# Fourteen units of the first layer's weights: the high and the low part made by GpSimd's casting and adding transfers instead of a VectorE subtraction

## The chip, the cores and the metric

The kernel runs on one core of one Trainium2 chip. The metric is the time of one launch on the device, in microseconds (us): the median of several executions. A profiled execution has its own time, and a span (first to last recorded instruction) that is a little shorter.

## The reference

A trunk of two layers over 256 latent tokens (a grid of 4 rows by 64) and 256 context tokens, both 1024 wide. What matters here is the first sub-layer, in which one projection feeds three branches:

```python
h = modulate(rmsnorm(x, norm1_g[l]), sh1, sc1)          # adaLN, the context stream likewise
p = h @ w_in[l]                                          # columns: a, g | q, k, v | gates
u = a * sigmoid(g); u = dwconv1d(u, dw, dw_b)            # 31 taps, depthwise
y_conv = silu(layernorm(u)) @ w_conv_out[l]
y_attn = merge_heads(neighbourhood_attention(q, k, v, k_c, v_c, rpb[l])) @ w_na_out[l]
x = x + g1 * (sigmoid(p_gc) * y_conv + sigmoid(p_ga) * y_attn) @ w_out[l]
```

The second sub-layer is a gated MLP (2816 wide) with a depthwise convolution of width 3. In the first layer the context tokens go through all of it as well, so its products run over 512 columns (256 latent, 256 context); in the second layer nearly all run over 256. All is fp32.

## The kernel before, in words

**Weights.** All weights of a layer lie in DRAM as 118 *units* of 128 partitions x 1024 fp32 (512 KB), each of them eight 128x128 tiles. Every product is made exact enough by splitting both operands into a high part in TensorE's type `fp32r` and the rest: `mm3` (L178) issues three matmuls per tile, high weight by high input (L179), high weight by low input (L180), low weight by high input (L181). A unit takes 24 matmuls of 128x512 in the first layer.

**Loading a unit** (`wparts` L150, `wunit` L170). SyncE (SP) issues one DMA into a `raw` tile (L157). ScalarE copies `raw` into `whi`, which rounds it to `fp32r` (L160). VectorE writes `wlo = raw - whi` (L161). `raw`, `whi` and `wlo` have four buffers each, which rotate; a buffer is taken again when the last reader of its old content is done. So the cast of a unit waits for the last L180 of the unit four places back, and the subtraction for its last L181. `unit8` (L193) returns the eight tile pairs of a unit, and `group` (L183) runs the 24 products of an output tile.

**The order of the work.** The program is written in the order in which TensorE is to work; the Tile framework then schedules each engine's instructions in an order of its own from that, and sets the waits. Every engine works through its list in order, so an instruction that waits holds up all behind it on the same engine. DMAs are issued by the engine on whose list they stand. Work of other kinds is put between the products by generators that `slot()` steps on (convolution taps, attention, adaLN products).

**Layer 0 up to the gates**, in the order of TensorE's work:

- x is loaded and its squares are summed; the adaLN rows for the first shift and scale come from products with the `wada` weights (L203, `sil` by `raw`). Then, for k = 0 to 7, `modulated` (L357) makes the high part of h on ScalarE (L366, 256 columns at a time) and the low part on VectorE (L367). TensorE makes the V products (L644) of that k and one or two GLU products of the first two GLU tiles (`glu0` L696, in the `sc` banks), and behind them the adaLN products for k+1.
- The 14 units U_IN to U_IN+13 follow in this order: Q0, K0, a1, g1, Q1, K1, a2, g2, Q2, K2, a3, g3, Q3, K3 (`qk` L749, `glu_groups` L617), with `in_group` (L614) calling `unit8`. Unit 14, the first gate (`gate` L624), is next and then 15 more of them. For Q and K, VectorE applies the rotation (L762 to L765), ScalarE makes their high part (L768) and VectorE the low part (L769); a Q also loads its bias of 640 KB (L760).
- Between those groups runs the attention (class at L385). A step makes the scores (L440) into the two `sc` banks and into `pt` and `main`; VectorE adds the bias and takes the row's minimum (L458); ScalarE takes the exponential (L461) and divides by the sum (L464). Some groups later `turn` (L486) transposes the probabilities on TensorE (L494, L499), ScalarE copies them out of PSUM into `pT` (L495 latent, L500 context), and `values` (L504) multiplies with V. PSUM has four `main` banks, two `sc`, one `pt`, one `po`.
- VectorE also does the convolution's taps (L589, L591), two per slot, each 128x512. `layer_norm` (L832) starts when all four tiles `cb_0` to `cb_3` are done; its first two sums are on GpSimd (L842 of `cb_0` and `cb_1`, L843).
- Later come adaLN dot products on VectorE (L271) with a row `sb` that is loaded by SP (L253) and goes through SiLU on ScalarE (L255).

GpSimd does little: memsets at the start, the powers for the norms' roots (L346), and L842/L843. It issues no DMA in the kernel before.

Of the kernel before, what the change touches and what calls it, by code (L numbers as in the profile page):

```python
# [8 lines left out]
F32 = mybir.dt.float32  # L9
F32R = mybir.dt.float32r  # L10
BF16 = mybir.dt.bfloat16
AF = mybir.ActivationFunctionType
ALU = mybir.AluOpType
AX = mybir.AxisListType

P = 128
# [15 lines left out]
UW = 1024  # L32
# [5 lines left out]
U_GLU0, U_V, U_IN, U_NA, U_CO, U_WO, U_UP, U_DN = 0, 2, 6, 36, 40, 44, 52, 96  # L38
# [7 lines left out]
def trunk(ctx: ExitStack, tc: tile.TileContext, xt, cvec, crow, wall, wada, params, bias_t, rope_t, out):  # L46
    nc = tc.nc
    pe, act, dve, pool, sp = nc.tensor, nc.scalar, nc.vector, nc.gpsimd, nc.sync
# [4 lines left out]
    wp = ctx.enter_context(tc.tile_pool(name="w", bufs=1))  # L53
# [6 lines left out]
    def nm(s):  # L60
        uid[0] += 1
        return f"{s}_{uid[0]}"
# [80 lines left out]
    lastdma = [None]  # L143
# [6 lines left out]
    def wparts(l, u, at=None, cuts=2):  # L150

        r = wp.tile([P, UW], F32, tag="raw", bufs=4, name=nm("raw"))
        hi = (at or wp).tile([P, UW], F32R, tag="whi", bufs=4, name=nm("whi"))
        lo = (at or wp).tile([P, UW], F32R, tag="wlo", bufs=4, name=nm("wlo"))
        cs = [slice(i * UW // cuts, (i + 1) * UW // cuts) for i in range(cuts)]
        for c in cs:
            lastdma[0] = sp.dma_start(r[:, c], wall[l, u][:, c])  # L157

        def split(c):
            act.copy(hi[:, c], r[:, c])  # L160
            dve.tensor_tensor(lo[:, c], r[:, c], hi[:, c].bitcast(F32), ALU.subtract)  # L161

        def more():
            for c in cs[1:]:
                split(c)

        split(cs[0])
        return (hi, lo), more

    def wunit(l, u, at=None, cuts=1):  # L170
        w, more = wparts(l, u, at, cuts)
        more()
        return w

    def cols(w, i):
        return sl(w[0], i), sl(w[1], i)
# [6 lines left out]
    def group(ps, ws, xh, xl, c):  # L183
# [6 lines left out]
        slot()  # L190
        return ps

    def unit8(l, u, at=None):  # L193
        w = wunit(l, u, at)
        return [cols(w, i) for i in range(KD)]


# [360 lines left out]
    for l in range(DEPTH):  # L558
# [5 lines left out]
        with ExitStack() if last else start as e1a:  # L564
# [49 lines left out]
            def in_group(t, c, tag="main"):  # L614
                return group(psum(tag), unit8(l, U_IN + t), *h1, c)
# [17 lines left out]
            with ExitStack() as e1b:  # L633
# [15 lines left out]
                if l == 0:  # L649
# [27 lines left out]
                    def more():  # L677
                        act.copy(wg[0][:, cuts[0]], rg[:, cuts[0]])
                        act.copy(pb, ps)
                        act.copy(wv[0][:, cuts[1]], rv[:, cuts[1]])  # L680
                        act.copy(wg[0][:, cuts[1]], rg[:, cuts[1]])
                        for w, r, c in ((wv, rv, cuts[0]), (wg, rg, cuts[0]), (wv, rv, cuts[1])):
                            low_part(w, r, c)
# [132 lines left out]
            with ExitStack() as e1c:  # L816
# [108 lines left out]
                for n in range(NB):  # L925
                    ps = group(psum(), unit8(l, U_WO + n), *z, ALL)
                    for s in range(NS):
                        residual(sss[s], ps, 2, n, s, s * S)
                    if last:
                        plain(n)  # L930
                    elif n == 0:
                        pace[0] = 0.8
                pace[0] = 0.3
                held = [unit8(l, U_WO + n) for n in range(NB, KD)]
                for s in range(NS if held else 0):
                    for n, w in zip(range(NB, KD), held):
# [13 lines left out]
        with ExitStack() as e2:  # L950
# [45 lines left out]
            if last:  # L996
# [14 lines left out]
                for i, ps in enumerate(pss):  # L1011
                    b = small([P, 1], "wb", 4)
                    act.copy(b, ps[:, S : S + 1])
                    u = ef.tile([P, S], F32, name=f"u{l}_{i}")
# [32 lines left out]
            for i in range(2, KF):  # L1047
                w = [unit8(l, ups[2 * i + t]) for t in range(2)]
# [176 lines left out]
```

## Time and profile before

| | |
|---|---|
| median of 3 runs | 1128.44 us (1127.71 to 1128.83) |
| the profiled execution | 1127.64 us, its span 1125.9 us |
| granted TensorE clock, mean | 0.998 of full speed |
| TensorE's weight loads (beside its matmuls) | 963.0 us busy, 86% of the span |
| moved by DMA | 190.83 MB, 169 GB/s over the span |

The profile puts every instruction under the source line that issued it. A row of groups names the line, the engine, the operation and its tiles as out<-in, how many there are (x244), their busy time and the mean of one in ns, then the engine's idle time just before them and who ended most of it. PE is TensorE, PEld its weight loads, DVE VectorE, ACT ScalarE, POOL GpSimd, SP SyncE; a q behind the name of an engine is its queue, which issues DMAs. A row of the order of time begins with the start of an instruction and its duration, both in us, and ends, in brackets, with the idle time before it and its releaser. For a DMA the second number is the time from issue to landing in the list of transfers, and the issue's own in the list of instructions. A row of windows gives, behind its bounds, the length of the stretch and each engine's busy time in it.

### The profile page before, as it was taken

The numbers are of one execution on the slowest core, as the hardware profiler recorded it, in microseconds if no ns is written. First come the engines' busy times: TensorE is split into PE (matmuls) and PEld (weight loads), VectorE is DVE, ScalarE is ACT, GpSimd is POOL, SyncE is SP. The second block draws the span as 40 slices with busy tenths as digits, with TensorE's granted clock in tenths as the row PEclk, the third lists the DMA queues.
The fourth block names the chain that finished last, engine by engine and source line by source line (L and its number), as shares of the span: only waits on it lengthen the run. The fifth ranks groups of instructions, "written<-read, shape, count | busy, mean of one in ns | idle before, by whom it ended". The sixth has DMA issues, their size and how long they took to land.

```text
span 1125.9 us, 17731 instructions
## 1 busy us (share of the span) xinstructions
PE 1114.1 (99%) x6828; PEld 963.0 (86%) x6828; DVE 908.3 (81%) x1631; ACT 563.6 (50%) x934; POOL 14.7 (1%) x24
## 2 busy tenths in 40 slices
PE   9999999999999999999999999999999999999997
PEld 7778777787789988888888888989888999999997
DVE  5689999685778788888898555789996898988773
ACT  4347657542333543434343222544677667766642
POOL 0000000000000000000000000000000000000000
PEclk9999999999999999999999999999999999999999
DMA  9833231536734354554556665556433575565781
GB/s 364 282 94 103 75 118 38 206 97 214 245 118 138 114 161 150 168 169 149 168 171 215 219 191 186 180 181 187 145 126 121 167 250 163 188 194 181 219 268 58
DMA packets 53941, 190.83 MB, mean 169 GB/s; under 512 B 6240, under 2 KB 6496, under 8 KB 53856
## 3 DMA queue, kind: packets, MB, share of 16 engines
q1 hardware_dynamic: 53568, 189.65, 52.1%
q8 instruction: 54, 0.88, 0.3%
q14 instruction: 31, 0.25, 0.1%
q10 hardware_dynamic: 288, 0.04, 0.0%
HBM read 188.62 MB, written 1.05 MB: 168 GB/s over the span
## 4 chain that ended last, share of the span: by engine, by line
PE 83%; DVE 9%; issue 6%; ACT 2%; DMA 0%; POOL 0%; POOLq 0%; DVEq 0%; SPq 0%; ACTq 0%
PE main L179 24%; PE main L181 24%; PE main L180 24%; DVE cb L591 4%; PE main L644 4%; DVE wlo L161 1%; PE sc L181 1%; PE sc L179 1%; PE sc L180 1%; PE po L202 1%; PE po L512 1%; PE sc L129 1%; PE sc L440 0%; DMA sb<-in_crow 0%; PE sc L494 0%
## 5 line engine op out<-in xcount | busy, mean ns | idle before, releaser
L179 PE MATMUL main<-h,whi 128*128 128x256 f32 (+1 forms) x1328 | 446.7, 337 | 0.0
L181 PE MATMUL main<-h,wlo 128*128 128x256 f32 (+1 forms) x1328 | 442.9, 335 | 1.0 <-DVE wlo L161 1.0
L180 PE MATMUL main<-h,whi 128*128 128x256 f32 (+1 forms) x1328 | 442.2, 334 | 0.1
L160 ACT CAST whi<-raw 128x1024 fp32r<-128x1024 f32 (+1 forms) x244 | 252.3, 1039 | 285.5 <-PE main L180 131.5
L161 DVE TENSOR_TENSOR wlo<-raw,whi 128x1024 fp32r<-128x1024 f32 (+1 forms) x244 | 292.9, 1207 | 112.5 <-ACT whi L160 108.0
L179 PEld LDWEIGHTS main<-h,whi 128*128 128x128 f32 x1328 | 249.4, 188 | 32.1 <-issue 3.6
L181 PEld LDWEIGHTS main<-h,wlo 128*128 128x128 f32 x1328 | 249.3, 188 | 29.6 <-DVE wlo L161 1.5
L180 PEld LDWEIGHTS main<-h,whi 128*128 128x128 f32 x1328 | 249.8, 188 | 28.5 <-DVE h L367 0.5
L591 DVE SCALAR_TENSOR_TENSOR cb<-u,par,cb 128x512 f32<-128x512 f32 (+1 forms) x240 | 140.4, 609 | 1.4
L271 DVE CUSTOM_DVE_ANT_0 t<-raw,sb,par 128x1024 bf16<-128x1024 f32 x100 | 126.7, 1277 | 1.0 <-ACT sb L255 0.7
L179 PE MATMUL main<-fh,whi 128*128 128x256 f32 (+1 forms) x386 | 123.0, 319 | 0.0
L180 PE MATMUL main<-fl,whi 128*128 128x256 f32 (+1 forms) x386 | 122.9, 319 | 0.0
L181 PE MATMUL main<-fh,wlo 128*128 128x256 f32 (+1 forms) x386 | 122.9, 318 | 0.0
L180 PEld LDWEIGHTS main<-fl,whi 128*128 128x128 f32 x386 | 72.7, 188 | 5.6
L179 PEld LDWEIGHTS main<-fh,whi 128*128 128x128 f32 x386 | 72.7, 188 | 5.6
L181 PEld LDWEIGHTS main<-fh,wlo 128*128 128x128 f32 x386 | 72.7, 188 | 5.5
L963 ACT ACTIVATE t<-main,par 128x512 f32<-128x512 f32 (+1 forms) x82 | 50.6, 667 | 39.0 <-PE main L181 39.0
L964 DVE SCALAR_TENSOR_TENSOR t<-main,par,t 128x510 f32<-128x510 f32 (+1 forms) x82 | 47.5, 615 | 10.2 <-ACT t L963 9.8
L967 DVE SCALAR_TENSOR_TENSOR t<-main,par,t 128x510 f32<-128x510 f32 (+1 forms) x82 | 46.6, 609 | 0.0
L366 ACT ACTIVATE h<-t,mod 128x256 fp32r<-128x256 f32 x56 | 25.4, 502 | 36.1 <-DVE t L365 36.1
L898 DVE SCALAR_TENSOR_TENSOR x<-main,mod,x 128x256 f32<-128x256 f32 x48 | 22.1, 479 | 23.5 <-PE main L181 23.3
L644 PE MATMUL main<-whi,h 128*128 128x512 f32 x128 | 40.6, 402 | 0.1
(221 smaller groups left out, 1188.2 us busy)
## 6 DMA issues: line engine op xcount, KB each, us to landing
raw<-in_wall SPq DMA_DIRECT2D x239, 512.0 KB, 4.2
raw<-in_wada SPq DMA_DIRECT2D x88, 512.0 KB, 4.3
bias<-in_bias_t SPq DMA_DIRECT2D x8, 640.0 KB, 4.8
row<-in_wada SPq DMA_DIRECT2D x8, 512.0 KB, 4.7
sb<-in_crow SPq DMA_DIRECT2D x5, 512.0 KB, 6.0
x<-in_xt SPq DMA_DIRECT2D x8, 256.0 KB, 4.4
raw<-in_wall SPq DMA_DIRECT2D x8, 256.0 KB, 7.1
out<-t SPq DMA_DIRECT2D x3, 256.0 KB, 2.1
```

What stands on the lines that cost most here:

```text
L160: act.copy(hi[:, c], r[:, c])
L161: dve.tensor_tensor(lo[:, c], r[:, c], hi[:, c].bitcast(F32), ALU.subtract)
L179: pe.matmul(ps, w[0], xh, start=start, stop=False)
L180: pe.matmul(ps, w[0], xl, start=False, stop=False)
L181: pe.matmul(ps, w[1], xh, start=False, stop=stop)
L271: dve.tensor_tensor_reduce(tmp().bitcast(BF16), r, v, 1.0, pr(l, BADA + n, 1), ALU.mult, ALU.add, mods[l][:, n, s : s + 1])
L366: high = act.activation(hi[:, c], y[:, c], AF.Identity, bias=b)
L591: dve.scalar_tensor_tensor(cb[j], src, w, cb[j], ALU.mult, ALU.add)
L644: mm = pe.matmul(pv[t], h1[n == 1][k][:, c], w[n == 2][:, b], start=k + n == 0, stop=k == KD - 1 and n == 2)
L963: act.activation(c, pv_, AF.Identity, bias=pr(l, FDB + t, 1), scale=w[1])
L964: dve.scalar_tensor_tensor(c[:, :, 1:], pv_[:, :, : S - 1], w[0], c[:, :, 1:], ALU.mult, ALU.add)
L967: dve.scalar_tensor_tensor(c[:, :, : S - 1], pv_[:, :, 1:], w[2], c[:, :, : S - 1], ALU.mult, ALU.add)
```

## The change

For layer 0's units U_IN to U_IN+13, `unit8` calls a new helper, `wadd`, in place of `wunit`. It takes no `raw` tile. GpSimd issues a DMA from the fp32 weights in DRAM into the `fp32r` tile `whi`, and the DMA casts. ScalarE writes the negative of `whi` into `wlo`. GpSimd issues a second DMA of the same weights into `wlo`, which adds them to what stands there, so that `wlo` holds raw - whi. The weights of these units are therefore read twice from DRAM. SP's 14 loads, ScalarE's 14 casts and VectorE's 14 subtractions of these units go. `lastdma`, behind which the bias and the first other loads are issued, is now GpSimd's second transfer for these units. The Bacc object is made with `dynamic_dma_scratch_size=1024`, the descriptor memory per partition that is set aside for GpSimd's transfers.

```diff
@@ -190,8 +190,16 @@
         slot()
         return ps
 
+    def wadd(l, u):
+        hi = wp.tile([P, UW], F32R, tag="whi", bufs=4, name=nm("whi"))
+        lo = wp.tile([P, UW], F32R, tag="wlo", bufs=4, name=nm("wlo"))
+        pool.dma_start(hi, wall[l, u])
+        act.mul(lo, hi.bitcast(F32), -1.0)
+        lastdma[0] = pool.dma_start(lo, wall[l, u], accum_op=ALU.add)
+        return hi, lo
+
     def unit8(l, u, at=None):
-        w = wunit(l, u, at)
+        w = wadd(l, u) if l == 0 and U_IN <= u < U_IN + 14 else wunit(l, u, at)
         return [cols(w, i) for i in range(KD)]
 
@@ -1211,7 +1219,7 @@
-    nc = bacc.Bacc("TRN2", target_bir_lowering=False, num_devices=1)
+    nc = bacc.Bacc("TRN2", target_bir_lowering=False, num_devices=1, dynamic_dma_scratch_size=1024)
```

What the change does to the order on each engine, as the changed program is built (lines by the kernel before, u counts the 14 units from 0, Hu is the casting transfer, Nu the negation, Lu the adding transfer):

- GpSimd: H0 H1 L0 L1 H2 H3 L2 L3 H4 L4 H5 H6 L5 L6 H7 H8 L7 L8 H9 H10 L9 L10 H11 L11 H12 L12 H13, the add L842, L13. From u = 4 on, Hu waits for the last L180 of unit u-4, and Lu for Nu and the last L181 of unit u-4. H0 to H3 wait for readers of the V and GLU units that held the same buffers: H0 for the GLU product at 42.39 us (by the times before), H1 for the end of the V products of k = 5, H2 for those of k = 7, H3 for the last GLU products.
- ScalarE: N0 stands just ahead of the pair L366 of k = 6, N1 ahead of that of k = 7; N2 and N3 behind the first sigmoid (L606); N4 between the L768 of Q0 and K0; N5 and N6 ahead of the second sigmoid; N7 among the divisions L464; N8 and N9 around the L768 of Q1 and K1, N9 just ahead of four copies L495; N10 behind those; N11 ahead of the context's exponentials (L477); N12, N13 and then the cast of unit 14 just ahead of four copies L500.
- TensorE's order stays, but for a few L644 that change places. VectorE has the 14 subtractions less, and some taps and rotations change places. On SP the first bias load comes ahead of six `wada` loads behind which it stood before.

## The prediction

> **What bounds the kernel now.** I read the page first (which engine is full), then the stretches of 20 us around the change, then the order of time of ScalarE and TensorE at the places that the change touches.
>
> ```profile
> span 1125.9 us, 17731 instructions
> PE 1114.1 (99%) x6828; PEld 963.0 (86%) x6828; DVE 908.3 (81%) x1631; ACT 563.6 (50%) x934; POOL 14.7 (1%) x24
> L161 DVE TENSOR_TENSOR wlo<-raw,whi 128x1024 fp32r<-128x1024 f32 (+1 forms) x244 | 292.9, 1207 | 112.5 <-ACT whi L160 108.0
> L160 ACT CAST whi<-raw 128x1024 fp32r<-128x1024 f32 (+1 forms) x244 | 252.3, 1039 | 285.5 <-PE main L180 131.5
> bias<-in_bias_t SPq DMA_DIRECT2D x8, 640.0 KB, 4.8
> ```
>
> TensorE is full (99%). I number the 14 units 0 to 13 in the order of their use, and call H(u) GpSimd's casting transfer of unit u, N(u) its negation and L(u) its adding transfer. They run from about 60 to 154 us; the windows there:
>
> ```profile
> 0.00:20.00 20.00, 18.10 (x126) 15.23 (x127) 9.71 (x25) 8.73 (x17) 2.76 (x9) 1.00 0.93 350
> 40.00:60.00 20.00, 20.00 (x111) 14.59 (x111) 12.16 (x27) 9.79 (x18) 0.00 (x0) 1.00 0.63 217
> 60.00:80.00 20.00, 20.00 (x87) 16.15 (x86) 18.73 (x34) 7.47 (x10) 0.00 (x0) 1.00 0.35 101
> 100.00:120.00 20.00, 20.00 (x131) 16.15 (x130) 20.00 (x39) 16.72 (x34) 0.00 (x0) 1.00 0.44 138
> 140.00:160.00 20.00, 20.00 (x88) 16.15 (x87) 20.00 (x43) 10.78 (x19) 1.69 (x1) 1.00 0.37 113
> ```
>
> After the length come TensorE, its loads, VectorE, ScalarE, GpSimd, granted clock, DMA share and GB/s. VectorE has no idle time from 100 us on, but TensorE is at 20.00 of 20 in each stretch as well, at clock 1.00. VectorE is saturated without holding anyone up, so taking work from it can gain only what TensorE loses today. The one such wait that I find near the change is this, behind a ScalarE copy that stands behind two SiLUs:
>
> ```profile
> 205.86 1.28 ACT L255 ACT_TABLE_LOAD   x1 [3.47 <-DMA sb<-in_crow]
> 209.47 0.44 PE L228 MATMUL pt<-ident,t 128*128 128x128 f32 x2 [0.58 <-ACT t L221]
> ```
>
> **The change, part by part.** Removed: 14 subtractions at 1207 ns, 16.9 us of VectorE. By the rows above that is worth between 0 and 0.58 us: VectorE's subtractions just ahead of the `sb` loads free the queue slot on SP before those loads, and come earlier. I take half, **-0.3**.
>
> ScalarE: 14 casts become 14 negations of the same shape, 1.04 us each; no change in busy time, but each negation now waits for GpSimd's transfer instead of SP's, which was early.
>
> SP loses 14 loads. The first bias load (640 KB) now stands ahead of the adaLN weights that were issued at 18.77 and are used at 26.83:
>
> ```profile
> 18.77 3.87 SPq L147 DMA_DIRECT2D raw<-in_wada  x4
> 26.83 1.07 PE L202 MATMUL po<-raw,sil 128*32 128x256 f32 x16
> raw<-in_wall SPq DMA_DIRECT2D x8, 256.0 KB, 7.1
> DMA to landing us min/median/max: 3.2/4.2/8.6
> ```
>
> 640 KB at 350 GB/s are 1.9 us. Those weights have 8.06 us; if they take the 7.1 us of the loads of that stretch, 0.9 us are uncovered; if they take the median 4.2, nothing. Bounds 0 and 0.9, taken **+0.2**, near nothing, as only the second half of the pair is at risk.
>
> The new chain per unit is H, N, L. Two prices are in no row: how long GpSimd is held by one issue (g), and how long from there to landing (X for H, X' for L). Rows for g: SP's issue, and GpSimd's own instructions beside a full VectorE:
>
> ```profile
> 100.78 0.33 SPq L157 DMA_DIRECT2D raw<-in_wall  x1
> 13.12 1.02 POOL L346 TENSOR_TENSOR rs<-red,mhalf 128x4 f32<-128x4 f32 x1 [10.82 <-DVE red L344]
> 149.47 1.69 POOL L842 TENSOR_TENSOR ss<-cb,cb 128x512 f32<-128x512 f32 x1 [135.32 <-DVE cb L591]
> 185.46 1.30 POOL L843 TENSOR_TENSOR ss<-ss,cb 128x512 f32<-128x512 f32 x1 [34.30 <-DVE ri L479]
> 234.82 1.99 POOL L346 TENSOR_TENSOR rs<-red,mhalf 128x4 f32<-128x4 f32 x1 [48.06 <-DVE red L344]
> ```
>
> g lies between 0.33 and 1.99; I take 1.5, the mean of 1.30 and 1.69, because it is the same engine beside the same VectorE work. X: SP's median 4.2 less its 0.33 of issue, 3.87; bounds 2.87 (the 3.2 above less 0.33) and 8.3. X' reads the tile as well as the weights: another 512 KB at 350 GB/s, 1.5 us, so 5.37. N with its two handovers: 1.1.
>
> [...]
>
> One unit is 5.58 us of TensorE (65.40, 70.98 below are the ends of units 0 and 1). H(u) can't start before the end of unit u-4, and L(u) must land by unit u, 16.7 us or more later; g+X+1.1+g+X' is 13.3. So data in time is the normal case, and what costs is **ScalarE's and GpSimd's order**: what stands behind a negation that waits. I go through the places with the least room.
>
> (A) N0 and N1 stand ahead of the high parts of h for k=6 and k=7:
>
> ```profile
> 42.39 0.40 PE L180 MATMUL sc<-h,whi 128*128 128x512 f32 x1
> 47.56 1.05 ACT L160 CAST whi<-raw 128x1024 fp32r<-128x1024 f32 x1 [0.88 <-PE main L644]
> 49.09 0.91 ACT L366 ACTIVATE h<-t,mod 128x256 fp32r<-128x256 f32 x2 [0.48 <-DVE t L365]
> 50.25 0.74 PE L644 MATMUL main<-whi,h 128*128 128x512 f32 x2
> 54.66 0.91 ACT L366 ACTIVATE h<-t,mod 128x256 fp32r<-128x256 f32 x2 [3.85 <-DVE t L365]
> 55.23 0.73 PE L644 MATMUL main<-whi,h 128*128 128x512 f32 x2
> ```
>
> H0's buffer is free after the product at 42.39, say 42.7; H1's at 47.56. SP moves 217 GB/s here, so I add 1.0 to X (bounds 0 and the 4.4 between 4.2 and 8.6). N0 ends at 42.7+1.5+3.87+1.0+1.1 = 50.2, 1.1 after h was begun; its first half takes 0.5, and TensorE took it 0.7 after it was there: late by 0.4 at most. N1 ends at 55.0, 0.3 late, with no room. Part of the second is already paid by the first: **+0.5**.
>
> (B) H2 waits for the end of k=7, H3 for the GLU products:
>
> ```profile
> 58.18 1.05 ACT L160 CAST whi<-raw 128x1024 fp32r<-128x1024 f32 x1
> 59.77 1.05 ACT L160 CAST whi<-raw 128x1024 fp32r<-128x1024 f32 x1
> 65.40 1.06 ACT L160 CAST whi<-raw 128x1024 fp32r<-128x1024 f32 x1 [2.67 <-issue]
> 70.98 1.05 ACT L160 CAST whi<-raw 128x1024 fp32r<-128x1024 f32 x1 [1.84 <-PE main L180]
> ```
>
> N2 ends at 58.2+1.5+3.87+1.1 = 64.7, L2 lands at 64.7+1.5+5.37 = 71.57. Unit 2 begins at 70.98 and first reads the low tile with its third product, at 71.45: **+0.1**.
>
> (C) N8 and N9 stand ahead of the probability copies L495, which free the two `sc` banks for the next scores:
>
> ```profile
> 93.59 0.42 ACT L768 ACTIVATE qk<-t 128x256 fp32r<-128x256 f32 x1 [0.83 <-DVE t L765]
> 95.07 1.05 ACT L160 CAST whi<-raw 128x1024 fp32r<-128x1024 f32 x1 [1.06 <-PE main L180]
> 101.60 1.06 ACT L495 COPY pT<-sc 128x512 f32<-128x512 f32 x2
> 102.52 1.16 PE L440 MATMUL sc<-qk,qk 64*128 64x512 f32 x6
> ```
>
> H8 waits for unit 4's end, 95.07-5.58 = 89.49, and lands at 94.86; N8 ends at 96.0 (ScalarE is free from 94.0). In GpSimd's order L8 comes before H9: L8 until 97.5, H9 until 99.0, landed at 102.9, N9 done at 104.0. The copies began at 101.60 and the scores at 102.52, right behind them: **+2.4**. N10 then ends at about 107, when the shifted exponentials would start anyway: nothing.
>
> (D) N12, N13 and the cast of unit 14 stand ahead of the context copies L500:
>
> ```profile
> 126.11 0.43 ACT L768 ACTIVATE qk<-t 128x256 fp32r<-128x256 f32 x1
> 126.79 1.05 ACT L160 CAST whi<-raw 128x1024 fp32r<-128x1024 f32 x1 [0.25 <-PE main L180]
> 133.32 1.06 ACT L500 COPY pT<-sc 128x512 f32<-128x512 f32 x2
> 134.75 0.61 ACT L500 COPY pT<-main 128x512 f32<-128x512 f32 x1
> 136.92 0.39 PE L440 MATMUL main<-qk,qk 64*128 64x512 f32 x1
> ```
>
> H12 (unit 8's end, 126.79-5.58 = 121.2) lands at 126.6, N12 ends at 127.7, L12 holds GpSimd until 129.2, H13 until 130.7, landed 134.6, N13 done 135.7, the cast 136.8, the four copies (133.32 to 135.36 before) 138.8. TensorE wants the `main` bank at 136.92: **+1.9**.
>
> One thing hides for free: GpSimd's add L842 now stands ahead of L13. Before, it waited for the last tap of `cb_1`, at 149.47, while unit 13 starts about 148.9 (unit 11 begins behind the scores of 136.92, at some 137.7, and two units of 5.58 later comes unit 13). In the new VectorE order that tap follows the rotation of unit 9, near 129, so the add is done before N13. Without that cover L13 would land at 149.47+1.69+1.5+5.37 = 158.0, 8.7 us late.
>
> Sum: -0.3+0.2+0.5+0.1+2.4+1.9 = **+4.8 us**. The profiled execution took 1127.64 us (span 1125.9 and 1.74 around it), 0.80 below the median of 1128.44: 1132.4 for a like execution, **1133.2** as median.
>
> **Rivals.**
> 1. Not slower: the negations are never late. With g 0.33 and 4.2 to landing N9 ends at 100.8, before the copies' 101.60, and the copies (D) end at 136.3: all that is left is -0.1 us, or -0.6 with the whole `sb` wait, 1127.8 to 1128.4. It decides at (C): N8 then ends at 95.1, and 2g+X must stay under 5.5, that is g under 0.8 us. For it: SP's rows. Against: GpSimd's.
> 2. Slow transfers: casting, or adding, runs well below the copy's rate. With g 2.0, X 4.87, X' 6.37: (A) 1.9, (B) 3.1, (C) 5.8, (D) 5.4, with the small terms 16.1: 1144.5. Adding alone at twice X' makes (B) 5.4: 1138.5.
> [...]
> 4. The change undoes itself: L13 behind the add, as worked out, 1133.2+8.7 less (D)'s shift, about 1140.
>
> **How the numbers follow.** Forecast (some of A, C, D, +2.3 to +9) 0.52; rival 1, 0.22; rival 2, 0.16; rival 3, 0.07; rival 4, 0.03. 0.2% is 2.3 us, about what a measurement of this kernel can tell from no change. Faster by more needs more than TensorE's 0.58: 0.04, out of rival 1. Same: the rest of rival 1 and the edge of the forecast, 0.22. Slower: 0.74. The range takes in rival 1's lower end and rival 2's sum: 1127.7 to 1145.0; left out are 0.04 below and about 0.1 above.
>
> **What would show it.** GpSimd's transfers would show g and the landing; ScalarE's idle time before the negations should be charged to GpSimd's DMA, most at N9 and N13; TensorE should wait at the scores (L440) for L495 and L500, near 103 and 137 us, and at L644 near 55. VectorE should have gaps between 100 and 160 us. I would be wrong if TensorE waited on the low tiles (L181) instead, if the waits lay outside 40 to 160 us, or if TensorE's time per product changed.

## The result, and the profile after

The changed kernel took 1135.26 us (median of 3: 1134.70, 1135.26, 1139.41) against 1128.44: **+6.8 us**. The ratio, estimated from all runs and so not the quotient of the two medians, is 1.0073 with an interval of 1.0060 to 1.0087. The forecast was 1133.2, slower, by +4.8. The profiled execution took 1134.70 (span 1132.9), 7.06 more than that of before. Line numbers above 192 are higher by 8 in the changed kernel.

Its page: the span, the busy times, and the new transfers (count, KB, median us from issue to landing):

```profile
span 1132.9 us, 17755 instructions
PE 1116.7 (99%) x6828; PEld 963.2 (85%) x6828; DVE 898.1 (79%) x1617; ACT 564.5 (50%) x934; POOL 35.2 (3%) x52
whi<-in_wall POOLq DMA_DIRECT2D x14, 512.0 KB, 5.7
wlo<-in_wall POOLq DMA_DIRECT2D x14, 512.0 KB, 5.6
```

VectorE is busy for 10.2 us less, and the span is 7.0 us longer. What TensorE waited for, longest first (total, times, longest one), shows two waits on ScalarE that were not there:

```profile
PE sc L448 <- ACT pT L503: 4.2, 1, 4.2
...
PE main L652 <- ACT h L374: 0.7, 1, 0.7
```

In order of time, TensorE's rows of the changed kernel that answer to 50.25, 102.52 and 136.92 of before:

```profile
51.01 1.02 PE L652 MATMUL main<-whi,h 128*128 128x512 f32 x2 [0.70 <-ACT h L374]
...
107.83 1.79 PE L448 MATMUL sc<-qk,qk 64*128 64x512 f32 x6 [4.21 <-ACT pT L503]
...
112.22 0.39 PE L179 MATMUL main<-h,whi 128*128 128x512 f32 x1
...
144.46 0.39 PE L448 MATMUL main<-qk,qk 64*128 64x512 f32 x1
```

and the row of before that answers to 112.22, the fourth product behind the scores:

```profile
105.11 0.39 PE L179 MATMUL main<-h,whi 128*128 128x512 f32 x1
```

The lag (how much later than in the kernel before the same product starts) is 0.76 at the first, 5.31 at the scores, 7.11 at the fourth product behind them, 7.54 at the context's scores, and 7.0 at the end. So between the scores and 112.22 another 1.8 us go with no wait at all. The windows tell why (the same columns as in the prediction; behind GpSimd's busy time stands the granted clock):

```profile
100.00:120.00 20.00, 15.79 (x87) 12.30 (x87) 18.29 (x38) 13.79 (x26) 2.88 (x4) 0.91 0.77 180
...
108.00:110.00 2.00, 2.00 (x11) 1.48 (x12) 0.70 (x4) 2.00 (x4) 0.63 (x1) 0.68 0.38 29
110.00:112.00 2.00, 2.00 (x8) 1.16 (x5) 2.00 (x9) 2.00 (x6) 0.88 (x1) 0.50 0.97 168
112.00:114.00 2.00, 2.00 (x10) 1.65 (x9) 2.00 (x8) 2.00 (x6) 0.00 (x0) 0.96 1.05 164
```

**The clock** fell to 0.50 right behind the stop. The chain of work through this place, of the changed kernel (start, length, what):

```profile
98.49 0.55 POOL wlo L198
99.05 7.18 DMA whi<-in_wall
106.22 0.02 issue
106.25 0.03 ACT wlo L197
106.28 0.94 issue
107.21 0.58 ACT pT L503
107.79 0.04 issue
107.83 1.79 PE sc L448 x6
```

Read it from below: the scores began right behind the copies, the copies right behind a negation, the negation right behind the landing of H9. That is (C) of the prediction, link for link; but the landing took 7.18 us from the issue.

### The profile page after: what moved, and what is told of

The parts are those of the page before. It is cut to its first block, busy times and chain, and to the rows that moved or that the text cites. A ratio compares the mean times of both kernels' runs of the same rounds, so it can differ in the third digit from the quotient of the medians.

```text
span 1132.9 us, 17755 instructions
## 1 busy us (share of the span) xinstructions
PE 1116.7 (99%) x6828; PEld 963.2 (85%) x6828; DVE 898.1 (79%) x1617; ACT 564.5 (50%) x934; POOL 35.2 (3%) x52
## 4 chain that ended last, share of the span: by engine, by line
PE 85%; DVE 5%; ACT 3%; DMA 3%; issue 3%; POOL 0%; SPq 0%; DVEq 0%; POOLq 0%; ACTq 0%
PE main L179 25%; PE main L181 24%; PE main L180 24%; PE main L652 4%; DVE cb L599 2%; DMA whi<-in_wall 2%; DVE wlo L161 1%; PE sc L179 1%; PE sc L180 1%; PE sc L181 1%; PE po L520 1%; ACT whi L160 1%; PE sc L448 1%; DMA sb<-in_crow 1%; DMA x<-in_xt 1%
## 5 line engine op out<-in xcount | busy, mean ns | idle before, releaser
L181 PE MATMUL main<-h,wlo 128*128 128x256 f32 (+1 forms) x1328 | 443.0, 335 | 1.1 <-DVE wlo L161 1.1
L180 PE MATMUL main<-h,whi 128*128 128x256 f32 (+1 forms) x1328 | 442.5, 334 | 0.1
L160 ACT CAST whi<-raw 128x1024 fp32r<-128x1024 f32 (+1 forms) x230 | 237.9, 1040 | 260.9 <-DMA raw<-in_wall 136.3
L161 DVE TENSOR_TENSOR wlo<-raw,whi 128x1024 fp32r<-128x1024 f32 (+1 forms) x230 | 276.7, 1210 | 109.4 <-ACT whi L160 108.2
L181 PEld LDWEIGHTS main<-h,wlo 128*128 128x128 f32 x1328 | 249.4, 188 | 29.7 <-DVE wlo L161 1.5
L180 PEld LDWEIGHTS main<-h,whi 128*128 128x128 f32 x1328 | 249.9, 188 | 28.5 <-DVE h L375 0.5
L599 DVE SCALAR_TENSOR_TENSOR cb<-u,par,cb 128x512 f32<-128x512 f32 (+1 forms) x240 | 144.5, 625 | 2.3
L180 PE MATMUL main<-fl,whi 128*128 128x256 f32 (+1 forms) x386 | 122.9, 319 | 0.0
L181 PE MATMUL main<-fh,wlo 128*128 128x256 f32 (+1 forms) x386 | 122.9, 318 | 0.0
L180 PEld LDWEIGHTS main<-fl,whi 128*128 128x128 f32 x386 | 72.7, 188 | 5.6
L181 PEld LDWEIGHTS main<-fh,wlo 128*128 128x128 f32 x386 | 72.7, 188 | 5.5
L972 DVE SCALAR_TENSOR_TENSOR t<-main,par,t 128x510 f32<-128x510 f32 (+1 forms) x82 | 47.6, 616 | 10.5 <-ACT t L971 10.2
```

Of the source, the lines that this page charges most:

```text
L180: pe.matmul(ps, w[0], xl, start=False, stop=False)
L181: pe.matmul(ps, w[1], xh, start=False, stop=stop)
L599: dve.scalar_tensor_tensor(cb[j], src, w, cb[j], ALU.mult, ALU.add)
L972: dve.scalar_tensor_tensor(c[:, :, 1:], pv_[:, :, : S - 1], w[0], c[:, :, 1:], ALU.mult, ALU.add)
```

## The experiments

Each was run in five rounds or more beside the kernel before, whose medians were 1127.68, 1127.72 and 1127.67 us in the three groups; "before" means those.

**1. The waiting negation put behind the copies.**

```diff
-        act.mul(lo, hi.bitcast(F32), -1.0)
+        with tc.issue_after(behind[0].ins) if u == U_IN + T_K + 2 else ExitStack():
+            act.mul(lo, hi.bitcast(F32), -1.0)
...
-                self.done = act.mul(pp, pp, ri)
+                self.done = behind[0] = act.mul(pp, pp, ri)
```

> The changed kernel, with one order forced: unit 9's negation comes behind the division that follows the next scores, and so behind the four probability copies. All transfers stay as they are. Theory (ScalarE's order: the copies stood behind a negation that waited for GpSimd's transfer, and the stop then cost clock): the 4.21 us wait of the scores goes, the clock stays at 1.00 between 108 and 114 us, 1.7 us come back with it; left are 0.76 at k=6 and some tenths later: 1128.8 to 1130.0. Rival (the added traffic of 512 KB per unit and the adding packets hold everything up, wherever the negation stands): another wait of 3 to 4 us in its place, 1133 to 1135.

Measured: 1134.45 us, +6.8, ratio 1.0059 (1.0047 to 1.0071; 1133.17 to 1136.94). A miss: the 4.21 us wait is gone, but the time isn't. In the profiled execution, the longest of its five, TensorE waited 2.1 us for h at k=6, with the clock at 0.50 behind it, and further on only for 0.2 to 1.3 us at a time, at many places. The forced order also moved the negation further than past the copies: it began at 117.27. What was late at the scores was VectorE:

```profile
105.93 5.47 DVE L602 SCALAR_TENSOR_TENSOR cb<-u,par,cb 128x512 f32<-128x512 f32 x7
111.32 0.69 DVE L469 CUSTOM_DVE_ANT_1 sc<-sc,bias 128x512 f32<-128x512 f32 x1
```

Seven taps of the convolution stand in one piece ahead of the row's minimum, which began 4.8 us behind its scores (106.53). In the kernel before it did so 1.4 us behind them:

```profile
103.92 0.69 DVE L458 CUSTOM_DVE_ANT_1 sc<-sc,bias 128x512 f32<-128x512 f32 x1
```

**2. Thirteen units.**

```diff
-        w = wadd(l, u) if l == 0 and U_IN <= u < U_IN + 14 else wunit(l, u, at)
+        w = wadd(l, u) if l == 0 and U_IN <= u < U_IN + 14 and u != U_IN + T_K + 2 else wunit(l, u, at)
```

> The changed kernel, but unit 9 (K2) is loaded and split as before; 13 units go the new way. Theory (ScalarE's order at this one place): as with the forced order, 1128.8 to 1130.0, because 13 of 14 units cost nearly nothing. Rival (traffic): one fourteenth of the loss goes, 1134 to 1135.

Measured: 1133.06 us, +5.4, ratio 1.0052 (1.0040 to 1.0065; 1131.93 to 1136.96). Neither theory had it. The copies and the scores are in time (103.04), the clock is at 1.00, and TensorE waits in two other places:

```profile
PE pt L502 <- ACT pp L472: 1.5, 1, 1.5
PE sc L448 <- ACT pT L508: 1.2, 1, 1.2
```

The first is VectorE again, with four taps and a subtraction ahead of a late minimum:

```profile
102.98 1.21 DVE L161 TENSOR_TENSOR wlo<-raw,whi 128x1024 fp32r<-128x1024 f32 x1
104.12 3.10 DVE L599 SCALAR_TENSOR_TENSOR cb<-u,par,cb 128x512 f32<-128x512 f32 x4
107.14 0.69 DVE L466 CUSTOM_DVE_ANT_1 sc<-sc,bias 128x512 f32<-128x512 f32 x1
```

The cause is in the changed kernel as well. Seven taps stand ahead of the minimum there:

```profile
102.56 5.49 DVE L599 SCALAR_TENSOR_TENSOR cb<-u,par,cb 128x512 f32<-128x512 f32 x7
109.35 0.70 DVE L466 CUSTOM_DVE_ANT_1 sc<-sc,bias 128x512 f32<-128x512 f32 x1 [1.30 <-ACT pT L503]
```

The taps in front of it are not what makes the minimum late. Seven stand there in experiments 4 and 8 too, and there it begins 1.7 and 1.5 us behind its scores (102.67 and 103.52). The rows of experiment 8:

```profile
99.60 5.47 DVE L599 SCALAR_TENSOR_TENSOR cb<-u,par,cb 128x512 f32<-128x512 f32 x7
104.99 0.69 DVE L466 CUSTOM_DVE_ANT_1 sc<-sc,bias 128x512 f32<-128x512 f32 x1
```

What differs is when VectorE gets there. In the changed kernel the shuffle of K1's rotation comes at 99.56, in the kernel before at 95.81, and the lateness begins at the second sigmoid, which stands behind N5 and N6: N5 waited 5.84 us for its transfer, and N6, the first row here, another 1.06. Behind it come the sigmoid, VectorE's product with it, and the minimum of the scores before these:

```profile
85.17 1.06 ACT L197 ACTIVATE wlo<-whi 128x1024 fp32r<-128x1024 f32 x1 [1.06 <-DMA whi<-in_wall]
86.13 0.58 ACT L614 ACTIVATE t<-main 128x512 f32<-128x512 f32 x1
86.81 0.69 DVE L615 TENSOR_TENSOR u<-main,t 128x512 f32<-128x512 f32 x1 [0.53 <-ACT t L614]
87.42 0.69 DVE L466 CUSTOM_DVE_ANT_1 sc<-sc,bias 128x512 f32<-128x512 f32 x1
```

The same sigmoid and minimum in the kernel before:

```profile
83.10 0.58 ACT L606 ACTIVATE t<-main 128x512 f32<-128x512 f32 x1
84.37 0.69 DVE L458 CUSTOM_DVE_ANT_1 sc<-sc,bias 128x512 f32<-128x512 f32 x1
```

Both are 3.0 us later, of which TensorE's own lag is 1.0 (those scores began at 83.27 and 82.23). So this too is a negation that waits in ScalarE's order, handed on by VectorE. In experiment 8 the two negations are done by 78.1, and the sigmoid starts at 82.69.

But with the scores at 107.83 VectorE is even idle for 1.30 us: the stop hides it. The second wait is (D) of the prediction. So behind the stop of the changed kernel stand two more delays that it covers: there TensorE comes so late that VectorE and the context's copies are done in time.

**3. More descriptor memory.**

```diff
-    nc = bacc.Bacc("TRN2", target_bir_lowering=False, num_devices=1, dynamic_dma_scratch_size=1024)
+    nc = bacc.Bacc("TRN2", target_bir_lowering=False, num_devices=1)
```

> The changed kernel with the descriptor memory left at its default, 16 times as large; every engine's order is the same. Theory (unit 9's casting transfer took 7.2 us because GpSimd's transfers run one after the other, and the adding transfer of unit 8 stood ahead of it for 3.3 us): no difference, 1134 to 1136, and the casting transfer right behind an adding one still needs 6 to 7 us. Rival (it waited for room for its descriptors): it lands in 4 to 5 us, the wait of the scores falls below 2.5 us, and the time to 1130 to 1132.5.

Measured: 1135.61 us, +7.9, ratio 1.0068 (1.0056 to 1.0080). As the theory had it: the wait of the scores is 4.6 us, and H9 still takes 7.2 us, so it didn't wait for room:

```profile
99.30 7.19 DMA whi<-in_wall
```

**4. VectorE's relief alone.**

```diff
+    def wskip(l, u):
+        r = wp.tile([P, UW], F32, tag="raw", bufs=4, name=nm("raw"))
+        hi = wp.tile([P, UW], F32R, tag="whi", bufs=4, name=nm("whi"))
+        lastdma[0] = sp.dma_start(r, wall[l, u])
+        act.copy(hi, r)
+        return hi, hi
...
-        w = wunit(l, u, at)
+        w = wskip(l, u) if l == 0 and U_IN <= u < U_IN + 14 else wunit(l, u, at)
```

The kernel leaves out the low tile of these 14 units and reads the high one in its place.

> The kernel before without the 14 subtractions: the low tile of these units is left out and the high tile is used in its place, so the third product of these units is with the high part. No GpSimd transfer, no negation. It prices VectorE's relief alone. Theory (VectorE is full but holds no one up): 1127.8 to 1128.5, that is 0 to 0.6 us less than before. Rival (VectorE's load costs TensorE more than the one wait that the trace shows): 1126.5 or less.

Measured: 1128.79 us, +1.1, ratio 1.0010 (1.0001 to 1.0019). Not a gain but a loss of up to 2 us. TensorE is full in every window from 100 to 180 us; a wait comes near 192 us, at the transposes of the last context scores, which come later in the new order of VectorE and ScalarE (argued from their rows; no run tested it):

```profile
PE pt L506 <- ACT pp L489: 0.8, 1, 0.8
```

**5. The traffic alone.**

```diff
         w = wunit(l, u, at)
+        if l == 0 and U_IN <= u < U_IN + 14:
+            d = wp.tile([P, UW], F32R, tag="idle", bufs=2, name=nm("idle"))
+            pool.tensor_copy(d[:, 0:1], w[0][:, 0:1].bitcast(F32))
+            pool.dma_start(d, wall[l, u])
+            pool.dma_start(d, wall[l, u], accum_op=ALU.add)
...
-    nc = bacc.Bacc("TRN2", target_bir_lowering=False, num_devices=1)
+    nc = bacc.Bacc("TRN2", target_bir_lowering=False, num_devices=1, dynamic_dma_scratch_size=1024)
```

> The kernel before, with the 28 transfers on top: after each of the 14 casts GpSimd copies one column of the new high tile into a spare tile, then issues a casting and an adding transfer of the same unit into that tile, which nobody uses. Nobody waits for them; SP's loads, ScalarE's casts and VectorE's subtractions stay. Theory (what costs is the waiting in ScalarE's order, not the traffic): at most 1.5 us slower than before. Rival (traffic, or GpSimd's issue against VectorE): 3 us or more slower, by TensorE waits at low tiles or copies.

Measured: 1128.59 us, +0.9, ratio 1.0007 (0.9998 to 1.0016). The 28 transfers run in the same stretch, and TensorE has no idle time there; a window of it:

```profile
100.00:120.00 20.00, 20.00 (x131) 16.03 (x130) 20.00 (x38) 16.37 (x33) 3.50 (x6) 1.00 0.83 240
```

So here neither their traffic nor GpSimd's issue beside a full VectorE (20.00 of 20 us) cost anything by itself that can be told from no change, as long as nobody waits for the transfers; with that the experiment's rival falls.

**6. The casting transfer alone.**

```diff
-        pool.dma_start(hi, wall[l, u])
-        act.mul(lo, hi.bitcast(F32), -1.0)
-        lastdma[0] = pool.dma_start(lo, wall[l, u], accum_op=ALU.add)
+        r = wp.tile([P, UW], F32, tag="raw", bufs=4, name=nm("raw"))
+        lastdma[0] = sp.dma_start(r, wall[l, u])
+        pool.dma_start(hi, wall[l, u])
+        dve.tensor_tensor(lo, r, hi.bitcast(F32), ALU.subtract)
```

> Only the casting transfer is kept: SP loads the raw tile as before, GpSimd's transfer casts into the high tile, VectorE subtracts as before. ScalarE has neither cast nor negation for the 14 units, and waits for no transfer; VectorE waits for it, with the convolution's taps behind. Theory (ScalarE's order): within 1.5 us of before, no wait of the scores for the copies. Rival (traffic of a second read): 3 us slower or more. Should VectorE's waits reach TensorE, the wait would name its rotation, its row minimum or its low tile.

Measured: 1135.55 us, +7.8, ratio 1.0063 (1.0051 to 1.0076; 1131.19 to 1136.00). A miss: as slow as the whole change, where the theory had at most 1.5 us, though ScalarE waits for no transfer, and there is no adding one. VectorE waits in its place. The three links at k=6: the subtraction of unit 0 waits for H0, ScalarE's high part of h waits for VectorE behind it, TensorE waits for that, and then runs at half the clock:

```profile
50.66 1.23 DVE L199 TENSOR_TENSOR wlo<-raw,whi 128x1024 fp32r<-128x1024 f32 x1 [1.97 <-DMA whi<-in_wall]
```

```profile
52.71 0.91 ACT L375 ACTIVATE h<-t,mod 128x256 fp32r<-128x256 f32 x2 [6.44 <-DVE t L374]
```

```profile
53.27 1.33 PE L653 MATMUL main<-whi,h 128*128 128x512 f32 x3 [1.74 <-ACT h L375]
```

```profile
54.00:56.00 2.00, 2.00 (x6) 1.63 (x6) 1.28 (x2) 0.00 (x0) 0.00 (x0) 0.50 0.39 152
```

That is the larger part: the transposes of 100.68 before start at 105.01 here. The rest is lost further on, in two waits of 0.6 us near 117 us behind a minimum that VectorE reached late (110.51, 3.7 us behind its scores), and in one of 1.7 near 210 us, where the kernel before has 0.58.

**7. The adding transfer alone.**

```diff
-        pool.dma_start(hi, wall[l, u])
+        r = wp.tile([P, UW], F32, tag="raw", bufs=4, name=nm("raw"))
+        lastdma[0] = sp.dma_start(r, wall[l, u])
+        act.copy(hi, r)
         act.mul(lo, hi.bitcast(F32), -1.0)
-        lastdma[0] = pool.dma_start(lo, wall[l, u], accum_op=ALU.add)
+        pool.dma_start(lo, wall[l, u], accum_op=ALU.add)
```

> Only the adding transfer is kept: SP loads, ScalarE casts from the raw tile and then negates the high tile, GpSimd's transfer adds the weights. ScalarE has 14 instructions of 1.06 us more, but none of them waits for a transfer. Theory: 0.5 to 2.5 us slower (one more instruction ahead of each tight place, 1.06 us at k=6 and k=7 and ahead of the copies), no wait above 1.5 us. Rival (the adding transfers are the costly part, by their 3.6 us of the queue): as slow as the change, 6 us or more.

Measured: 1127.86 us, +0.1, ratio 1.0003 (0.9994 to 1.0012). Better than the theory's range: fourteen more instructions on ScalarE, 14 adding transfers (5.7 to 9.8 us to land) and 14 subtractions less on VectorE cost and bring nothing that can be told from no change. With 6 this splits the change: the loss comes with the casting transfer, which an engine waits for *in its order* (ScalarE in the change, VectorE in 6, so that the two losses are alike in size but not in place); behind the adding one nobody stands but TensorE, which reads the low tile much later.

**8. Five high buffers.** The three places where high tiles are made get `bufs=5` for `whi`:

```diff
-        hi = wp.tile([P, UW], F32R, tag="whi", bufs=4, name=nm("whi"))
+        hi = wp.tile([P, UW], F32R, tag="whi", bufs=5, name=nm("whi"))
```

> The changed kernel with five buffers for the high tiles instead of four, so that a casting transfer may start one unit (5.58 us) earlier; GpSimd then issues it ahead of the adding transfer of the unit before. Theory (the negation is late because its transfer starts late and stands behind an adding one): the wait of the scores falls from 4.2 to at most 1.5 us, the clock stays at 1.00 there, 1 to 4 us slower than before. Rival (lateness is that of the adding transfers or of traffic): still 6 to 7 us slower.

Measured: 1132.08 us, +4.4, ratio 1.0040 (1.0029 to 1.0052). H9 is now issued at 90.11 in place of 99.05, ahead of L8 (92.44), and N9 is done at 96.8 in place of 107.3. What stands ahead of the four copies is now N10, which stood behind them in the changed kernel; its transfer was issued at 95.69:

```profile
101.94 1.06 ACT L197 ACTIVATE wlo<-whi 128x1024 fp32r<-128x1024 f32 x1 [2.80 <-DMA whi<-in_wall]
```

```profile
PE sc L448 <- ACT pT L503: 2.3, 2, 1.7
```

Of the 2.3 us only 0.6 are at (C), with the clock at 1.00. The 1.7 are new, near 183 us, where no transfer of GpSimd is left: there an ordinary cast (L160) came to stand ahead of four copies, and behind this wait the clock fell to 0.61 and 0.53 in two windows of 2 us. So the remedy did what the theory said at its place, and the total missed its upper end of 4 us. It also shows why the casting transfer is late: it lands in the high tile itself and can't be issued before that buffer is free, while SP's load went into a `raw` tile ahead of time.

**9. ScalarE held up without any transfer.**

```diff
+                        if extra:
+                            for _ in range(extra.pop()):
+                                act.copy(tmp(), pt)
                         act.copy(pts[i][:, :, n * P : (n + 1) * P], pt.rearrange("p (k q) -> p k q", k=4))
```

with `extra = [8]` and `extra = [3]`, taken by the first of the copies.

> The kernel before, with no GpSimd transfer; ahead of the first four probability copies ScalarE copies the first scores' bank eight times more into spare tiles (about 0.5 us each, 3.9 us together). Theory (a late ScalarE at this place is the whole cause of the change's largest loss, and the stop then costs clock): the scores wait 3.5 to 4.2 us for the copies, the clock falls to 0.5 to 0.7 for some 4 us behind it, together 4.5 to 6.5 us slower. Rival (it took the transfers for that: traffic in the same microseconds, or GpSimd): the wait is made good by the slack behind it, or the clock stays at 1.00: at most 4 us slower.

> As with eight, but three copies (about 1.5 us). Theory: the scores wait 1.2 to 1.6 us; a stop this short may leave the clock at 1.00, then 1.2 to 1.8 us slower. If the clock falls behind a short stop as well, 2.5 to 3.5 us slower.

Measured: eight copies 1133.06 us, +5.4, ratio 1.0044 (1.0032 to 1.0057); three copies 1129.34, +1.7, ratio 1.0015 (1.0007 to 1.0024). Both sums came as expected, the form only in part: products of the next unit were scheduled ahead of the scores, so these didn't wait; with eight copies TensorE waited 2.6 us for a division some ten us later, and there the clock fell with no GpSimd transfer in the program:

```profile
PE pt L496 <- ACT pp L466: 2.6, 1, 2.6
```

```profile
118.00:120.00 2.00, 2.00 (x10) 1.48 (x12) 2.00 (x4) 2.00 (x5) 0.00 (x0) 0.64 0.00 0
120.00:122.00 2.00, 2.00 (x22) 2.00 (x22) 1.27 (x3) 1.41 (x2) 0.00 (x0) 0.51 0.00 0
```

ScalarE also loaded its function table once more than before (1.28 us, at 114.29, among the divisions), so the 5.4 us are not the price of 3.9 us alone. What the run shows is that a late ScalarE at this place stops TensorE, and that the clock falls behind the stop, with no transfer of GpSimd. With three copies the profile has no wait that the kernel before doesn't have; where these 1.7 us go is not shown.

**10. Without units 0 and 1**, with four and with five high buffers:

```diff
-        w = wadd(l, u) if l == 0 and U_IN <= u < U_IN + 14 else wunit(l, u, at)
+        w = wadd(l, u) if l == 0 and u in range(U_IN, U_IN + 14) and u not in (U_IN + T_Q, U_IN + T_K) else wunit(l, u, at)
```

> The changed kernel without units 0 and 1, which are loaded and split as before; 12 units go the new way. Theory (units 0 and 1 cost through the high parts of h at k=6 and k=7, by 0.7 us in the profiled execution and by 2 us and a drop of the clock in others): no wait at k=6 and k=7, 4.5 to 6.5 us slower than before, and a narrower spread than the 1134.7 to 1139.4 of the change. Rival (these two are harmless): as slow as the change, 7 us.

> Without units 0 and 1 and with five buffers for the high tiles: both remedies together. Theory: what is left are short waits of the scores, 1 to 4 us slower than before; it can't be faster than before, because the 12 subtractions that VectorE is spared are worth nothing. Rival (VectorE's relief pays once the waits are gone): 1 us or more faster than before.

Measured: four buffers 1135.83 us, +8.2, ratio 1.0064 (1.0050 to 1.0078; 1134.34 to 1136.10); five buffers 1132.06, +4.4, ratio 1.0034 (1.0021 to 1.0046). The first misses its range: the wait at k=6 is gone, the spread is narrow as expected, but the scores now wait longer, and the clock stays down longer behind them:

```profile
PE sc L448 <- ACT pT L503: 4.8, 1, 4.8
```

```profile
112.00:114.00 2.00, 2.00 (x6) 1.52 (x5) 2.00 (x8) 2.00 (x5) 0.00 (x0) 0.50 1.08 182
```

They start at 107.73, as good as at the changed kernel's 107.83: the end of this stop is set by the chain of transfers and negations, not by TensorE, so what is saved at (A) is waited for at (C). The second is past the upper end of its range of 1 to 4, and its rival falls: VectorE's relief brings no gain there, though a wait of 1.9 us near 183 us is left, as in experiment 8. No version here beats the kernel before; the nearest is the adding transfer alone, level with it.

## Why the prediction was right, and where its terms were not

Direction, mechanism and range held; the sum was 2.3 us low against the profiled execution (7.06 for 4.8). That it came so near is in part luck: it had no term for the clock (1.8), had (C) too small by 1.8, and had 1.9 at (D) that isn't there.

- **VectorE's relief, -0.3: nothing.** Experiment 4 measured a loss, by its interval of 0.1 to 2.1 us, and no run shows a gain. That VectorE "is saturated without holding anyone up" was right of its load.
- **Not in the sum: N5 and N6 ahead of the second sigmoid.** The prediction went through N0 to N3, N8, N9, N12 and N13 as the places with the least room, and expected the longest idle times at N9 and N13. They were 4.13 and 2.50 us there, and 5.84 ahead of N5. Through the sigmoid that made VectorE late: the shuffle of Q1's rotation came at 94.25 in place of 91.15 and that of K1's at 99.56 in place of 95.81. This is the largest delay which the prediction didn't see. In the changed kernel the stop covers it; in experiments 1 and 2 it shows.
- **The first bias load, +0.2:** no loss is seen ahead of 50 us; the lag at 51.01 is 0.76, and 0.70 of it is the wait for h.
- **(A) +0.5: right**, 0.70. It differs from execution to execution (2.1 in that of experiment 1), and with a drop of the clock behind it, it may be what the third run of 1139.41 shows (clock 0.993 against 0.997); no trace of that run exists.
- **(B) +0.1:** no wait.
- **(C) +2.4: the right place, link for link, mis-sized: 4.2, and 1.8 for the clock.** H9's issue began at 99.05, where the prediction had 97.5, because N8 didn't start at 94.9 but at 97.03, behind Q1's high part, which waited for that late rotation, and with the 0.76 of (A) in it; and H9 landed 7.18 later, where g and X made 5.37. Together 3.4 us, half of them by the price of the transfer. The hold g alone was the other way off: 0.55 us for a casting transfer (0.87 to 0.91 right behind an adding one) and 0.88 for an adding one, in place of 1.5. I had GpSimd's issue as the thing that orders the transfers; what makes them wait comes behind the issue. From issue to landing, casting transfers over all (min, median, max), the one of unit 12 at 128.47 with nothing ahead of it, and the adding ones:

```profile
DMA to landing us min/median/max: 3.6/5.7/7.2
```

```profile
DMA to landing us min/median/max: 3.6/3.6/3.6
```

```profile
DMA to landing us min/median/max: 5.4/5.6/6.2
```

  The six that were issued within 2 us of an adding one took 6.4 to 7.2. Experiment 3 rules out room for descriptors. That a casting one starts when the adding one ahead of it is nearly through is inferred from these times; no run changed that order alone, and an adding one is not needed to make it slow. In experiment 8 the four adding ones that were issued 1.5 to 2.3 us behind a casting one, from 84.66 to 103.42, took 7.4 to 7.9. In experiment 6, with no adding transfers, the median of the casting ones is 4.5, but the one of 94.19, beside two loads of SP (93.03 and 94.42), took 7.2.
- **(D) +1.9: hardly anything**, 0.4 between 112.22 and 144.46. The last copy L508 began at 143.96, and the scores stood at its heels. It was added to (C) as if both could be paid; a stop at (C) gives the transfers behind it time. Without that stop (experiment 2) the wait is there, with 1.2.
- **The add L842** was hidden, as forecast: it started at 135.97, ahead of L13 at 142.11.
- **The rivals.** Hidden: no; g was under its 0.8, but 2g+X, with 0.55 for L8 and 7.18 for H9, was 7.7 in place of less than 5.5. Slow transfers: in part; the casting ones behind an adding one were slow, the adding ones themselves, with 5.6, faster than the 6.87 of the sum, and nobody waited on a low tile. Rival 3 (0.07), GpSimd's issue made longer by VectorE: no; at 0.55 us it was shorter beside the full VectorE than any of GpSimd's rows before, and experiment 5 ran all 28 issues for +0.9. The change undoing itself: no.

## What to carry to other kernels

An instruction that waits costs what stands behind it on its engine (here a wait of 4.21 us at the scores, behind N9 and the copies), so when work moves to a slower path, ask of each new wait what is next in that engine's order; whether the transfer itself is fast enough for its reader is the smaller question. Places where two engines hand over within half a microsecond didn't add up here: the first stop paid for the next, and mending one uncovered the other, so weigh such places in the order of time and not as a plain sum. And a wait travels: VectorE came late because, some 20 us earlier, a sigmoid that it needed stood behind two negations on ScalarE that had waited 5.84 and 1.06 us. Before the order of a late engine is blamed, follow it back to the first thing that it waited for.

## What the runs showed of the hardware

- **Behind five stops of TensorE, of 1.7 to 4.2 us, the granted clock fell, and each time TensorE missed about 1.7 us by it.** The stops were of 4.2 (the changed kernel), 2.6 (experiment 9), 2.1 (experiment 1), 1.74 (experiment 6) and 1.7 us (experiment 8), and the clock fell to 0.50 to 0.53 in a window of 2 us. What it missed comes to 1.7 us over the windows (0.32, 0.50 and 0.04 of 2 us each in the changed kernel), which is 3.4 us at half speed; behind the stop of 4.8 us (experiment 10) it was twice as much (0.13, 0.50, 0.50, 0.50 and 0.08 of 2 us each). By the lag of the products behind it the price in the changed kernel was 1.8 us (7.11 for 5.31). Behind a stop of 2.0 us (experiment 5, at 210 us), one of 1.9 (the last kernel of experiment 10) and one of 1.5 (experiment 2) the clock stayed at 1.00. So near 2 us the outcome was mixed, and no run shows what decided it.
- **For 512 KB an adding transfer of GpSimd took 5.4 to 6.2 us in the changed kernel; a casting one took 3.6 to 6.1, and 6.4 to 7.2 within 2 us behind an adding one.** An adding one issued 1.5 to 2.3 us behind a casting one took 7.4 to 7.9 (experiment 8).
- **GpSimd's issue took 0.55 us for a casting transfer and 0.88 us for an adding one** beside a VectorE that was busy 18.29 of 20 us (100 to 120 us). Five casting issues right behind an adding one took 0.87 to 0.91, the first of all took 0.76, and none of the changed kernel's 28 took longer than 0.91 us.
